# A transformer block on one core: the row of token scales sent to all partitions through HBM instead of by diagonals and matmuls

## The chip, the cores and the metric

The kernel runs on one core of a Trainium2 chip. The metric is the device time of one execution in microseconds (us). Five engines work side by side, each through its own list of instructions in order: TensorE (PE in the profile, with PEld for its weight loads), VectorE (DVE), ScalarE (ACT), GpSimd (POOL) and SyncE (SP), which here only issues DMAs. An engine waits for another by semaphores. GpSimd can issue DMAs too, on a queue of its own.

## The reference

A block with 256 tokens of 2048 features (all float32):

```python
h = rmsnorm(x, norm1_g)                        # per token: x * rsqrt(mean(x*x) + eps) * g
q, k, v, u = split(h @ w_in)                   # 12 query heads, 4 key/value heads, Fourier width 512
a = rmsnorm(window_attention(q, k, v, sink), attn_out_g)
f = rmsnorm(fourier_mix(u, w_fourier), fourier_out_g)
x = x + concat([a, f]) @ w_out
h = rmsnorm(x, norm2_g)
gate, val = split(h @ w_up)                    # 5504 columns each
gate = conv3(gate, dw_w) + dw_b                # along the tokens, each feature by itself
x = x + (gelu(gate) * val) @ w_down
y = rmsnorm(x, normf_g)
```

Each rmsnorm has one scale per token, 1/sqrt(mean square). Such a scale commutes with the matmul behind it, so the kernel multiplies the unscaled rows by the weights and applies the scale to the result.

## The kernel before, in words

**Products.** Every float32 product is split into three in a faster format: a weight tile `raw` becomes `hi` (a rounded copy, made by ACT in line 168) and `lo` (the rest, made by DVE in line 169), the tokens likewise, and PE adds hi·hi, lo·hi and hi·lo in PSUM. `split(i)` does this for the weight tile `i`, a "unit" of 128x2048, and then issues the load of unit `i + 3` on SP's queue (line 152), since there are three `raw` buffers. `hi` and `lo` also have three buffers each.

**Order.** All instructions are written out by hand in the order in which they are issued on each engine; no scheduler moves them. In the first part (attention, Fourier, output projection) `unit(i, work)` issues what is listed in `before[i]`, the matmuls of unit `i`, what is listed in `beside[i]`, the split of unit `i + 2`, and what is listed in `behind[i]`. In the second part (up-projection, convolution, down-projection) `ff_step(n)` does the same around item `n`: `beside[n]`, the split of item `n + 2`, `behind[n]`. Items 0, 1, 2, ... are gate 0, value 0, gate 1, value 1, gate 2, value 2 and so on; each is 32 matmuls by `still_weights` (line 319), 16 that use `hi` and 16 that use `lo`, in turn.

**Two layouts of the scale.** `rstd_of` (line 261) leaves the scales of the 256 tokens as a tile of 128 partitions x 2: token b·128+p sits in partition p, column b. DVE makes `var` (line 264) and POOL raises it to the power -0.5 (line 267). Where the result of a product has tokens along the partitions, this form is used directly. Where the result has features along the partitions and the tokens along the free dimension (the keys, and gate and value), the scale is needed as a row of 256 numbers that is the same in all 128 partitions: `r1b` for the first rmsnorm, `r2b` for the second.

**How the row is made before.** `spread_diagonals` (line 276) has DVE multiply the identity `ident` by each of the two columns, which gives two 128x128 diagonal matrices in a buffer of the tag `junk`. `spread_sums` (line 283) has PE multiply a matrix of `ones` by each diagonal (line 286); every row of the result in PSUM is then the row of scales. Each of these two products of float32 shows as two matmuls in the trace, so four for a row. DVE copies the result to SBUF: `r1b` in line 569, `r2b` in line 293.

**Where that stands.** For `r1b` the three pieces are spread over the steps: diagonals behind unit 6, matmuls before unit 8, copy beside unit 8; the first reader is the first key's `qk_out` (line 604), beside unit 9. For `r2b` all stands in one place (line 1126): after the matmuls of items 0 and 1 have been issued, DVE reduces the sums of squares (line 1125), `rstd_of` follows, then the diagonals, the matmuls and the copy, and then `ff_step(1)`, which splits item 3. PE goes on with item 2.

**Readers of r2b.** `scaled_sum` (line 829) adds the two halves of a finished item out of PSUM (ACT copies one half, DVE adds the other, line 833, which frees the PSUM bank) and multiplies by `r2b` (line 834). `gate_conv` (line 837) then works on the result: ACT in line 841, DVE in lines 842 and 845. `up_posts` (line 984) places these: the sum of item n beside n + 1, the convolution beside n + 2.

**GpSimd's list.** Around the two places it has the powers of line 267, additions of squares (line 456) in the first part, and from item 13 on DMAs that add weights (lines 947, 949, 958).

Of the kernel before, what the change touches and what calls it, by code (L numbers as in the profile page):

```python
# [8 lines left out]
F32 = mybir.dt.float32  # L9
F32R = mybir.dt.float32r  # L10
AF = mybir.ActivationFunctionType
ALU = mybir.AluOpType

P = 128
D = 2048
S = 256
# [76 lines left out]
def block_kernel(  # L93
# [18 lines left out]
    nc = tc.nc  # L112
# [3 lines left out]
    wp = ctx.enter_context(tc.tile_pool(name="wp", bufs=1))  # L116
    mm = ctx.enter_context(tc.tile_pool(name="mm", bufs=4, space=bass.MemoryType.PSUM))
    dn = ctx.enter_context(tc.tile_pool(name="dn", bufs=4, space=bass.MemoryType.PSUM))
# [4 lines left out]
    def bank(pool, name):  # L123
        return pool.tile([P, 512], F32, tag=pool.name, name=name)
# [115 lines left out]
    ones = base.tile([P, P], F32, tag="ones", name="ones")  # L240
# [3 lines left out]
    ident = base.tile([P, P], F32, tag="ident", name="ident")  # L244
    make_identity(nc, ident)

    ps = bank(dn, "ps_warm")
# [25 lines left out]
            junk, t[:, b, :], AF.Square, accum_out=parts[:, b, c : c + 1]  # L273
        )

    def spread_diagonals(r, name):
        t = wp.tile([P, 512], F32, tag="junk", name=f"diag{name}")
        dgs = [t[:, b * P : (b + 1) * P] for b in range(2)]
        for b, dg in enumerate(dgs):
            nc.vector.tensor_scalar(dg, ident, r[:, b : b + 1], None, ALU.mult)  # L280
        return dgs

    def spread_sums(dgs, name):
        ps = bank(dn, "ps_spread" + name)
        for b in range(2):
            nc.tensor.matmul(
                ps[:, b * P : (b + 1) * P], ones, dgs[b], start=True, stop=True
            )
        return ps

    def spread(r, dst, name):

        nc.vector.tensor_copy(dst, spread_sums(spread_diagonals(r, name), name)[:, :S])


    def moving_weights(hi, lo, n, kk, act, b, ps, first, last, q0=0):
# [45 lines left out]
    before, beside, behind = {}, {}, {}  # L342

    def at(when, i, f, *a):
        when.setdefault(i, []).append((f, a))
# [13 lines left out]
    for c in range(4):  # L359
        t = base.tile([P, 4, 512], F32R, tag=f"hT{c}", name=f"hT{c}")  # L360
        hT.append(t)
    ps_u = [bank(mm, f"ps_u{b}") for b in range(2)]
    for k in range(NK):
# [3 lines left out]
        n = 1 if c < 2 else 2  # L367
# [8 lines left out]
        if k < 4:  # L376

            for p, w in enumerate([hi, hi, lo]):
                for b in range(2):
# [3 lines left out]
                        start=k == 0 and p == 0, stop=False,  # L383
# [15 lines left out]
    r1 = base.tile([P, 2], F32, tag="rstd1", name="rstd1")  # L399
# [19 lines left out]
    def rows_out(hi, lo, ps):  # L419

        for b in range(2):
            r = r1[:, b : b + 1]
            nc.scalar.activation(hi[:, b, :], ps[b], AF.Copy, scale=r)
            nc.vector.scalar_tensor_tensor(
                lo[:, b, :], ps[b], r, f32(hi[:, b, :]), ALU.mult, ALU.subtract
            )
# [9 lines left out]
    r1b = ph.tile([P, S], F32, tag="r1b", name="r1b")  # L436
# [120 lines left out]
            nc.vector.tensor_scalar(rel[:, s], rel[:, s], rq_inv[:, b : b + 1], None, ALU.mult)  # L557
        nc.vector.tensor_scalar(sink_neg, vcol(V_SINK, NH), -1.0, None, ALU.mult)

    spread1 = {}  # L560
    at(beside, 5, fourier_positions)
    at(before, 6, fourier_weights)
    at(beside, 6, fourier_weights_out)
    at(behind, 6, lambda: spread1.update(d=spread_diagonals(r1, "1")))
    at(before, 7, fourier_rows)
    at(beside, 7, fourier_rows_out)
    at(before, 8, lambda: spread1.update(ps=spread_sums(spread1["d"], "1")))
    at(beside, 8, lambda: rows_out(v_hi, v_lo, ps_v))
    at(beside, 8, lambda: nc.vector.tensor_copy(r1b, spread1["ps"][:, :S]))
    at(behind, 8, distances)  # L570

    def fourier_channels_steps():
# [216 lines left out]
    for n, (c, kq) in enumerate(OUT_ORDER):  # L789
# [15 lines left out]
        if kq >= 2:  # L805
            part = "a" if kq == 2 else "f"
            ps = ps_a[c] if kq < 3 else ps_a[c, "f"]
# [18 lines left out]
    parts = {}  # L826
    gate_out, sums_of, act = {}, {}, {}

    def scaled_sum(ps, name):
        tmp = fp.tile([P, S], F32, tag="ftmp", name=f"ft_{name}")  # L830
        nc.scalar.activation(tmp, ps[:, S : 2 * S], AF.Copy)  # L831
        add = fp.tile([P, S], F32, tag="fadd", name=f"fa_{name}", bufs=3)
        nc.vector.tensor_tensor(add, ps[:, 0:S], tmp, ALU.add)  # L833
        nc.vector.tensor_tensor(add, add, r2b, ALU.mult)
        sums_of[name] = add

    def gate_conv(j):
        ga = sums_of.pop(f"g{j}")
# [144 lines left out]

    def up_posts(n, kind, j, ps):
        if kind == "gate":
            at(beside, n + 1, scaled_sum, ps, f"g{j}")
            at(beside, n + 2, gate_conv, j)
            at(behind, n + 2, gate_gelu, j)
        else:
            at(beside, n + 1, scaled_sum, ps, f"v{j}")  # L990
            at(beside, n + 2, val_mult, j)
            if j % 8 == 7 and j < 8 * N_GROUPS:
                g = j // 8
                at(behind, n + 1, operand, g, "P1")
                at(behind, n + 2, operand, g, "N4")
                at(behind, n + 3, operand_sums, g, 0)
                at(behind, n + 4, operand, g, "P7")
                at(behind, n + 4, operand, g, "P2")
                at(behind, n + 5, operand_sums, g, 1)
                at(behind, n + 5, operand, g, "N5")  # L1000
                at(behind, n + 6, operand, g, "N3")
                at(behind, n + 7, operand, g, "P6")
            if j >= 8 * N_GROUPS:
                at(behind, n + 2, act_parts, j)
# [108 lines left out]
    for q in range(2):  # L1113
        kind, j = items[q]
        ps = bank(mm, f"ps_{kind}{j}")
# [8 lines left out]
    tot2 = base.tile([P, 2], F32, tag="tot2", name="tot2")  # L1124
    nc.vector.tensor_reduce(tot2, ssq2, mybir.AxisListType.X, ALU.add)
    spread(rstd_of(tot2, D, "2"), r2b, "2")
    ff_step(1)
    up_posts(1, *items[0], pair[0][0])
    up_posts(2, *items[1], pair[1][0])

    for n, it in enumerate(items):
# [8 lines left out]
        if it[0] in ("gate", "val"):  # L1140
            kind, j = it
            ps = bank(mm, f"ps_{kind}{j}")
            still_weights(*halves.pop(up_index[n]), ps, range(NK))
            ff_step(n)
            up_posts(n, kind, j, ps)
            continue
        if it[0] == "product":
            kind, g, c, p = it
# [3 lines left out]
            else:  # L1152
                ps = bank(mm, f"ps_{p}{g}{c}")
# [5 lines left out]
        else:  # L1159
            kind, g, c = it  # L1160
            hi, lo = halves.pop(up_index[n])
            ps = [bank(mm, f"ps_l{g}{c}{b}") for b in range(2)]
# [160 lines left out]
```

## Time and profile before

| | |
|---|---|
| time, median of 3 runs | 948.39 us (948.16 to 949.04) |
| the profiled execution's own time | 948.77 us |
| its span, first to last instruction | 947.0 us |
| TensorE (PE) | 937.1 us busy, 5085 matmuls |
| VectorE (DVE) | 750.0 us busy |
| ScalarE (ACT) | 534.2 us busy |
| GpSimd (POOL) | 43.3 us busy, 58 instructions |
| moved by DMA | 211.58 MB, mean 223 GB/s |

The page gives for each engine the time in which it was busy, and then the chain that ended last: the work followed back from the last instruction, each time to what released it. A timeline gives one line per instruction: start, duration, engine, line of the kernel, operation, result <- operands, and in brackets the idle time ahead of it and what ended it. PE's matmuls are pipelined: the next starts before the last one's duration is over, so the difference of two starts, and not a duration, says what a matmul takes of PE's time.

### The profile page before, as it was taken

How to read it: one execution, taken by the hardware profiler on the slowest of the kernel's cores; microseconds unless marked ns; L12 is line 12 of the kernel's file. 1: busy time of each engine (PE TensorE's matmuls, PEld its weight loads, DVE VectorE, ACT ScalarE, POOL GpSimd, SP SyncE). 2: the span in 40 equal slices, each digit the busy share in tenths (PEclk: the TensorE clock that was granted, in tenths of full speed). 3: DMA queues.
4: the chain of work that ended last, by engine and by line, in shares of the span. 5: the costliest groups of instructions: out<-in, count | busy, mean ns of one | idle time of the engine just before them, and what ended most of it. 6: DMA issues, size and time to landing. Idle time of an engine off the chain costs nothing.

```text
span 947.0 us, 12779 instructions
## 1 busy us (share of the span) xinstructions
PE 937.1 (99%) x5085; PEld 813.0 (86%) x5085; DVE 750.0 (79%) x935; ACT 534.2 (56%) x646; POOL 43.3 (5%) x58
## 2 busy tenths in 40 slices
PE   9999999999999999999999999999999999999996
PEld 7889998888888888888888888888888888888885
DVE  7758877666676689887898877988879979888775
ACT  7756766454454546556565555665556755553442
POOL 0000000000000000000000000000000000000003
PEclk9999999999999999999999999999999999999998
DMA  9844444446446675987778797877987787776542
GB/s 366 337 181 141 174 139 172 139 173 219 181 178 226 248 237 185 282 250 263 229 257 246 237 304 235 267 231 227 296 256 245 207 301 219 224 242 220 179 133 89
DMA packets 32108, 211.58 MB, mean 223 GB/s; under 512 B 3504, under 2 KB 4016, under 8 KB 7984
## 3 DMA queue, kind: packets, MB, share of 16 engines
q1 hardware_dynamic: 28448, 184.55, 52.4%
q0 software_dynamic: 3600, 26.22, 14.7%
q8 instruction: 40, 0.66, 0.3%
q14 instruction: 20, 0.16, 0.0%
HBM read 208.65 MB, written 2.10 MB: 223 GB/s over the span
## 4 chain that ended last, share of the span: by engine, by line
PE 98%; DVE 1%; DMA 0%; issue 0%; ACT 0%; POOL 0%; POOLq 0%; DVEq 0%; ACTq 0%
PE ps_gate L319 25%; PE ps_val L319 25%; PE ps_q L319 7%; PE ps_P L1051 3%; PE ps_P L1053 3%; PE ps_P L1052 3%; PE ps_a L304 2%; PE ps_k L319 2%; PE ps_a L302 2%; PE ps_a L303 2%; PE ps_N L1051 2%; PE ps_N L1053 2%; PE ps_N L1052 2%; PE ps_l L303 2%; PE ps_l L302 2%; PE ps_l L304 2%
## 5 line engine op out<-in xcount | busy, mean ns | idle before, releaser
L169 DVE TENSOR_TENSOR lo<-raw,hi 128x2048 fp32r<-128x2048 f32 (+1 forms) x133 | 302.7, 2276 | 54.0 <-ACT hi L168 54.0
L168 ACT ACTIVATE hi<-raw 128x2048 fp32r<-128x2048 f32 (+1 forms) x133 | 253.1, 1903 | 59.2 <-PE ps_l L303 24.9
L319 PE MATMUL ps_gate<-hU,hi 128*128 128x512 f32 x688 | 236.2, 389 | 0.0
L319 PE MATMUL ps_val<-hU,hi 128*128 128x512 f32 x688 | 236.2, 389 | 0.0
L319 PE MATMUL ps_gate<-hU,lo 128*128 128x256 f32 x688 | 189.9, 276 | 0.0
L319 PE MATMUL ps_val<-hU,lo 128*128 128x256 f32 x688 | 189.9, 276 | 0.0
L319 PEld LDWEIGHTS ps_gate<-hU,hi 128*128 128x128 f32 x688 | 129.2, 188 | 26.8
L319 PEld LDWEIGHTS ps_val<-hU,hi 128*128 128x128 f32 x688 | 129.1, 188 | 26.8
L319 PEld LDWEIGHTS ps_gate<-hU,lo 128*128 128x128 f32 x688 | 129.1, 188 | 1.1
L319 PEld LDWEIGHTS ps_val<-hU,lo 128*128 128x128 f32 x688 | 129.2, 188 | 1.1
L831 ACT ACTIVATE ft_g<-ps_gate 128x256 f32<-128x256 f32 x43 | 16.5, 384 | 120.0 <-PE ps_gate L319 119.8
L319 PE MATMUL ps_q<-hT,hi 128*128 128x512 f32 x192 | 66.2, 392 | 0.0
L831 ACT ACTIVATE ft_v<-ps_val 128x256 f32<-128x256 f32 x43 | 16.5, 384 | 88.0 <-PE ps_val L319 88.0
L319 PE MATMUL ps_q<-hT,lo 128*128 128x256 f32 x192 | 52.5, 277 | 0.0
L1051 PE MATMUL ps_P<-hi_P,op_P 128*128 128x512 f32 x128 | 49.8, 389 | 0.0
L1052 PE MATMUL ps_P<-hi_P,op_P 128*128 128x512 f32 x128 | 49.8, 389 | 0.0
L1053 PE MATMUL ps_P<-lo_P,op_P 128*128 128x512 f32 x128 | 49.8, 389 | 0.0
L943 DVE TENSOR_TENSOR lo_N<-sumw,hi_N 128x2048 fp32r<-128x2048 f32 x16 | 36.6, 2290 | 10.2 <-ACT hi_N L942 10.2
L319 PEld LDWEIGHTS ps_q<-hT,hi 128*128 128x128 f32 x192 | 35.8, 188 | 7.0
L302 PE MATMUL ps_a<-hi,cat 128*128 128x512 f32 x96 | 37.9, 395 | 0.0
L304 PE MATMUL ps_a<-lo,cat 128*128 128x512 f32 x96 | 37.5, 391 | 0.0
L833 DVE TENSOR_TENSOR fa_g<-ps_gate,ft_g 128x256 f32<-128x256 f32 x43 | 18.2, 422 | 24.3 <-ACT ft_g L831 24.3
(332 smaller groups left out, 1606.0 us busy)
## 6 DMA issues: line engine op xcount, KB each, us to landing
raw<-in_w_up SPq DMA_DIRECT2D x86, 1024.0 KB, 5.2
raw<-in_w_in SPq DMA_DIRECT2D x20, 1024.0 KB, 4.8
raw<-in_w_out SPq DMA_DIRECT2D x16, 1024.0 KB, 4.8
sumw<-in_w_down POOLq DMA_DIRECT2D x16, 1024.0 KB, 8.7
raw<-in_w_down_late SPq DMA_DIRECT2D x8, 1024.0 KB, 4.8
raw<-in_w_down_last SPq DMA_DIRECT2D x4, 768.0 KB, 4.2
ux<-in_w_u_x SPq DMA_DIRECT2D x3, 768.0 KB, 9.3
xs<-in_x SPq DMA_DIRECT2D x4, 512.0 KB, 16.1
```

Of the source, the lines that this page charges most:

```text
L168: nc.scalar.activation(hi[:, 0:n], raw[:, 0:n], AF.Copy)
L169: nc.vector.tensor_tensor(lo[:, 0:n], raw[:, 0:n], f32(hi[:, 0:n]), ALU.subtract)
L302: nc.tensor.matmul(ps, ah, wh, start=first and q == q0, stop=False)
L303: nc.tensor.matmul(ps, al, wh, start=False, stop=False)
L304: nc.tensor.matmul(ps, ah, wl, start=False, stop=last and q == q0 + len(kk) - 1)
L319: nc.tensor.matmul(ps[:, x], (hi, lo)[i][:, k * P : (k + 1) * P], hk(k)[:, x], start=n == 0 and k == 0, stop=n == len(order) - 1 and k == ...
L831: nc.scalar.activation(tmp, ps[:, S : 2 * S], AF.Copy)
L833: nc.vector.tensor_tensor(add, ps[:, 0:S], tmp, ALU.add)
L943: nc.vector.tensor_tensor(lo, src, f32(hi), ALU.subtract)
L1051: nc.tensor.matmul(ps, o[:, 0, p, :], hi[:, s], start=first and p == 0, stop=False)
L1052: nc.tensor.matmul(ps, o[:, 1, p, :], hi[:, s], start=False, stop=False)
L1053: nc.tensor.matmul(ps, o[:, 0, p, :], lo[:, s], start=False, stop=last and p == 3)
```

## The change

The row of scales goes by way of HBM. POOL issues two DMAs: the first writes the 128x2 tile to a tile `row` of 2x128 numbers in HBM, element by element in the order of the tokens; the second, which waits for the first, reads these 256 numbers into each of the 128 partitions. The diagonals, the matmuls and the copies are gone, for `r1b` and for `r2b`. For `r1b` both DMAs stand behind unit 6. For `r2b` they stand where `spread` stood; besides, the first reader is moved: `scaled_sum` of gate 0 leaves out the multiplication by `r2b`, which is done in `row_scale` beside item 3, after the split of item 4, ahead of gate 0's convolution. All other readers stay as they are.

```diff
-    def spread_diagonals(r, name):
-        t = wp.tile([P, 512], F32, tag="junk", name=f"diag{name}")
-        dgs = [t[:, b * P : (b + 1) * P] for b in range(2)]
-        for b, dg in enumerate(dgs):
-            nc.vector.tensor_scalar(dg, ident, r[:, b : b + 1], None, ALU.mult)
-        return dgs
-
-    def spread_sums(dgs, name):
-        ps = bank(dn, "ps_spread" + name)
-        for b in range(2):
-            nc.tensor.matmul(
-                ps[:, b * P : (b + 1) * P], ones, dgs[b], start=True, stop=True
-            )
-        return ps
+    rows = ctx.enter_context(tc.tile_pool(name="rows", bufs=1, space=bass.MemoryType.DRAM))
 
     def spread(r, dst, name):
 
-        nc.vector.tensor_copy(dst, spread_sums(spread_diagonals(r, name), name)[:, :S])
+        row = rows.tile([2, P], F32, tag="row" + name, name="row" + name)
+        nc.gpsimd.dma_start(row.rearrange("b p -> p b"), r)
+        nc.gpsimd.dma_start(dst, row.rearrange("b p -> (b p)").partition_broadcast(P))
...
-    spread1 = {}
     at(beside, 5, fourier_positions)
     at(before, 6, fourier_weights)
     at(beside, 6, fourier_weights_out)
-    at(behind, 6, lambda: spread1.update(d=spread_diagonals(r1, "1")))
+    at(behind, 6, spread, r1, r1b, "1")
     at(before, 7, fourier_rows)
     at(beside, 7, fourier_rows_out)
-    at(before, 8, lambda: spread1.update(ps=spread_sums(spread1["d"], "1")))
     at(beside, 8, lambda: rows_out(v_hi, v_lo, ps_v))
-    at(beside, 8, lambda: nc.vector.tensor_copy(r1b, spread1["ps"][:, :S]))
     at(behind, 8, distances)
...
-    def scaled_sum(ps, name):
+    def scaled_sum(ps, name, late=False):
         tmp = fp.tile([P, S], F32, tag="ftmp", name=f"ft_{name}")
         nc.scalar.activation(tmp, ps[:, S : 2 * S], AF.Copy)
         add = fp.tile([P, S], F32, tag="fadd", name=f"fa_{name}", bufs=3)
         nc.vector.tensor_tensor(add, ps[:, 0:S], tmp, ALU.add)
+        sums_of[name] = add
+        if not late:
+            row_scale(name)
+
+    def row_scale(name):
+        add = sums_of[name]
         nc.vector.tensor_tensor(add, add, r2b, ALU.mult)
-        sums_of[name] = add
...
         if kind == "gate":
-            at(beside, n + 1, scaled_sum, ps, f"g{j}")
+            at(beside, n + 1, scaled_sum, ps, f"g{j}", j == 0)
+            if j == 0:
+                at(beside, n + 2, row_scale, "g0")
             at(beside, n + 2, gate_conv, j)
             at(behind, n + 2, gate_gelu, j)
```

## The prediction

> **What bounds the kernel now.** I read the busy times first, then the chain that ended last, then PE's list of waits.
>
> ```profile
> span 947.0 us, 12779 instructions
> PE 937.1 (99%) x5085; PEld 813.0 (86%) x5085; DVE 750.0 (79%) x935; ACT 534.2 (56%) x646; POOL 43.3 (5%) x58
> ...
> PE 98%; DVE 1%; DMA 0%; issue 0%; ACT 0%; POOL 0%; POOLq 0%; DVEq 0%; ACTq 0%
> ```
>
> ```profile
> PE ps_warm L249 <- POOL ones L241: 1.0, 1, 1.0
> PE ps_u L381 <- ACT hT L256: 0.4, 1, 0.4
> ```
>
> PE is 98% of the chain, and its whole list of waits is the second fence: two, 1.4 us together, both at the very start. So from then on to its last matmul PE runs without a pause, and the end moves with PE's own work: a matmul taken out moves it by that matmul's share, and work of DVE, ACT, POOL or the DMAs counts only where it becomes late enough to stop PE.
>
> **What the change takes from PE.** Four matmuls for each row. Their price is read from the starts of the neighbours in PE's timeline (start, duration, instruction), first for r1b, then for r2b:
>
> ```profile
> 53.26 0.39 PE L303 MATMUL ps_v<-hi,hT 128*128 128x512 f32 x1
> 53.49 0.40 PE L304 MATMUL ps_v<-lo,hT 128*128 128x512 f32 x1
> 53.72 0.61 PE L286 MATMUL ps_spread<-diag,ones 128*128 128x128 f32 x4
> 54.17 0.61 PE L531 MATMUL ps_y<-uf,G 128*128 128x129 f32 x4
> ```
>
> ```profile
> 268.24 0.39 PE L319 MATMUL ps_val<-hU,hi 128*128 128x512 f32 x1
> 268.47 0.28 PE L319 MATMUL ps_val<-hU,lo 128*128 128x256 f32 x1
> 268.59 0.61 PE L286 MATMUL ps_spread<-diag,ones 128*128 128x128 f32 x4
> 268.95 0.48 PE L319 MATMUL ps_gate<-hU,hi 128*128 128x512 f32 x1
> 269.26 0.28 PE L319 MATMUL ps_gate<-hU,lo 128*128 128x256 f32 x1
> ```
>
> At r1b the spread holds PE from 53.72 to 54.17: 0.45 us; without it ps_y starts at 53.72, one pitch of L304 (0.23, as from 53.26 to 53.49) after it. At r2b the undisturbed pair has 0.23 us from a hi matmul to its lo matmul (268.24 to 268.47) and 0.12 from there to the next hi. So without the spread the gate's hi would start at 268.59 and its lo at 268.82; it starts at 269.26, which is 0.44 late. The two together: **0.9 us**, on the path.
>
> **What it takes from DVE** is off the path: the diagonals, the copies and one wait.
>
> ```profile
> 46.23 0.48 DVE L280 TENSOR_SCALAR diag<-ident,rstd 128x128 f32<-128x128 f32 x2
> ...
> 55.31 0.41 DVE L569 COPY r1b<-ps_spread 128x256 f32<-128x256 f32 x1
> ```
>
> ```profile
> 266.03 0.48 DVE L280 TENSOR_SCALAR diag<-ident,rstd 128x128 f32<-128x128 f32 x2 [0.80 <-POOL rstd L267]
> 269.23 0.42 DVE L293 COPY r2b<-ps_spread 128x256 f32<-128x256 f32 x1 [2.72 <-PE ps_spread L286]
> 269.57 2.28 DVE L169 TENSOR_TENSOR lo<-raw,hi 128x2048 fp32r<-128x2048 f32 x1
> 271.77 0.42 DVE L833 TENSOR_TENSOR fa_g<-ps_gate,ft_g 128x256 f32<-128x256 f32 x1
> 272.23 0.42 DVE L834 TENSOR_TENSOR fa_g<-fa_g,r2b 128x256 f32<-128x256 f32 x1
> 272.57 2.29 DVE L169 TENSOR_TENSOR lo<-raw,hi 128x2048 fp32r<-128x2048 f32 x1
> 274.77 0.48 DVE L842 SCALAR_TENSOR_TENSOR cv<-fa_g,vec,cv 128x255 f32<-128x255 f32 x1
> ...
> 277.27 2.29 DVE L169 TENSOR_TENSOR lo<-raw,hi 128x2048 fp32r<-128x2048 f32 x1
> ```
>
> That is 1.8 us of work and 2.72 us in which DVE sat waiting for PE's spread. No wait of PE names DVE, so I count them at nothing. The cover is PE's own distance to the next tile that it needs, worked out below.
>
> **What it adds: two DMAs in a row on POOL, and a wait of DVE.** POOL computes the scales and then issues both; the second waits for the first. What starts, and what stands behind in POOL's list:
>
> ```profile
> 35.95 0.71 POOL L267 TENSOR_TENSOR rstd<-var,half_pow 128x2 f32<-128x2 f32 x1 [34.47 <-DVE var L264]
> 69.20 0.75 POOL L456 TENSOR_TENSOR sq_f<-sq_f,sq 128x256 f32<-128x256 f32 x1 [32.55 <-ACT sq L455]
> ...
> 265.31 0.69 POOL L267 TENSOR_TENSOR rstd<-var,half_pow 128x2 f32<-128x2 f32 x1 [64.73 <-DVE var L264]
> ```
>
> ```profile
> 336.51 1.05 POOL L958 DMA_DIRECT2D rawd00b<-in_w_down  x1 [70.52 <-DVE cv L842]
> ```
>
> POOL's next work is 32 us behind the first pair and 70 us behind the second, so POOL's own waiting holds up nobody. SP's queue is not passed by anything: its loads follow DVE's splits as before.
>
> What one such DMA takes, from issue to landing, the trace doesn't show: nothing in it writes single 4-byte elements to HBM, and nothing this small is issued by POOL. The nearest rows (tile, queue, KB, us to landing; then a POOL issue's own time in ns):
>
> ```profile
> gfb<-in_normf_g POOLq DMA_DIRECT2D x1, 1024.0 KB, 4.8
> ...
> out_y<-xs SPq DMA_DIRECT2D x2, 128.0 KB, 1.9
> ```
>
> ```profile
> rawd10b<-in_w_down POOLq DMA_DIRECT2D x1, 1024.0 KB, 10.1
> ```
>
> ```profile
> L1168 POOL DMA_DIRECT2D gfb<-in_normf_g x1: 568/568/568, 839.8 to 839.8; - x1
> ```
>
> The low end is 1.9 us each (SP, 128 KB, the size of the second DMA), the high end 10.1 us each (POOL's slowest, which adds 1 MB in place). I take 4.8 us each, gfb's: it is the one plain DMA from POOL, and like the second one it repeats an HBM row to all partitions, though eight times as many bytes. Its issue took POOL 0.57 us, which lies within. The pair is then 9.6 us, with ends at 3.8 and 20.2.
>
> The Trainium skill's page "DMA: Bandwidth & Descriptors", section "Anatomy of one DMA — SWDGE (gpsimd) path", gives about 2.0 us plus the bytes at 436 GB/s per DMA; by it the pair would take an estimated 4.3 us, near the low end, and the sum would be the same. The gfb row, 4.8 us for 1 MB, agrees with its 4.4.
>
> **r1b.** The scales are ready at 35.95 + 0.71 = 36.7; r1b lands at 46.3, or at 56.9 by the high end. Its first reader:
>
> ```profile
> 61.18 0.42 DVE L604 TENSOR_TENSOR add_k<-add_k,r1b 128x256 f32<-128x256 f32 x1
> ```
>
> That is 60.7 once PE is 0.45 us earlier. It is in time by either end: no cost.
>
> **r2b** is the one to watch. All of the following is the time of before less 0.45. The scales are ready at 265.31 + 0.69 - 0.45 = 265.55. DVE now does: the split of item 3 as soon as ACT's half is there, the sum of gate 0 (which frees the PSUM bank and doesn't need r2b), the split of item 4, then the late multiplication. ACT's and PE's rows for it:
>
> ```profile
> 267.31 1.91 ACT L168 ACTIVATE hi<-raw 128x2048 fp32r<-128x2048 f32 x1 [2.87 <-PE ps_gate L319]
> ...
> 272.68 0.60 ACT L841 ACTIVATE cv<-fa_g,vec 128x256 f32<-128x256 f32 x1 [1.38 <-DVE fa_g L834]
> ```
>
> ```profile
> 285.36 0.39 PE L319 MATMUL ps_val<-hU,hi 128*128 128x512 f32 x1
> 285.59 0.28 PE L319 MATMUL ps_val<-hU,lo 128*128 128x256 f32 x1
> ```
>
> Item 3's split starts at 267.31 + 1.91 - 0.45 = 268.8; with DVE's pitches above (2.20 for a split, 0.46 for the sum, 2.20 for the next split) it reaches the multiplication at **273.7**. r2b lands at 265.55 + 9.6 = 275.2 (ends 269.4 and 285.8). So DVE probably waits some 1.5 us here, in place of the 2.72 that it waited before.
>
> Behind that multiplication on DVE stand gate 0's convolution, the sums of value 0 and gate 1, and the split of item 5, value 2. If the multiplication starts at T, ACT's convolution part begins 0.45 later and takes 0.60, DVE goes on about 0.05 behind that, and from there it is 277.27 - 274.77 = 2.50 to the split and 2.29 through it: item 5 is ready at T + 5.9. PE needs its lo at 285.59 - 0.9 = 284.7. So PE stops only if r2b lands after **278.8**, 13.2 us behind the scales. With 9.6 there are 3.6 us to spare. The cost is nothing; by the high end it would be 285.8 - 278.8 = 7.0 us.
>
> **The sum.** Against the profiled execution, 947.0 of span and 1.8 around it, 948.8 in all: minus 0.9. It stands 0.4 above the median of the runs (948.39); the same difference there gives **947.5 us**, 0.1% less. A measurement of this kernel can tell about 0.2% (1.9 us) from no change, so this counts as no change.
>
> **The rivals.**
>
> *The second row is late (slower).* The place is DVE's late multiplication, with item 5's split behind it; it decides from 13.2 us for the pair on. At 10.1 us each PE stops for 7.0 us: 948.39 - 0.9 + 7.0 = 954.5. For it: 256 elements of 4 bytes are a kind of write of which the trace has no row, and two landings stand one behind the other. Against: POOL's 10.1 is for 1 MB that is added in place, and DMAs have room there, as the row below shows (columns: stretch and length, then busy time and count of PE, PEld, DVE, ACT, POOL, then granted clock, DMA share, GB/s).
>
> ```profile
> 268.00:274.00 6.00, 6.00 (x38) 5.37 (x37) 4.73 (x5) 4.17 (x5) 0.00 (x0) 1.00 0.19 41
> ```
>
> A variant is that descriptors of POOL's DMAs wait for DVE's splits: one split of 2.29 us ahead of each DMA adds 4.6, so r2b lands at 279.8 and PE stops for 1.0, which gives 948.5, still within 0.2%. The Trainium skill, page "SBUF — State Buffer", section "Who interferes with whom", has DVE shut GpSimd out for a whole instruction, but only copies, casts and tensor_scalar in their two-port modes, and it notes that tensor_tensor did not stall DMAs. By that the variant falls; no row of before can show it.
>
> *Nothing is gained: 948.4.* PE's 0.9 us comes back as a wait, if the stream of split weights and not PE sets the pace, or if ps_y and the gate start no earlier. For it: PE would be 0.9 us closer to every load and split. Against: PE's list has no wait for DVE, ACT or a DMA after the start, and the item at 285.36 had its split done at 279.6.
>
> *More is gained.* If DVE's time did set the pace somewhere, its 2.72 of idle time goes too: 948.39 - 0.9 - 2.72 = 944.8. The same list speaks against it.
>
> **How the numbers follow.** The forecast has 0.79; nothing gained 0.08; late row 0.09; more gained 0.04. The forecast and the second give "within 0.2%", 0.87; late row is slower, 0.09; more gained is faster, 0.04. The range runs from 946.8 (the forecast less 0.45, an error of half the PE term, and less the 0.2 by which the fastest run lies below the median) to 949.1 (nothing gained, plus the 0.65 by which the slowest run of before lies above its median); it takes in the short stop of 1.0 us, and leaves out the full late row and the larger gain.
>
> **What will show it.** In the profile after: PE's busy time about 1 us less, its waits still two, ps_y 0.23 us behind the last L304, and the gate 0.12 behind the last value matmul. r2b's multiplication for gate 0 starts between 273.7 and 276, with an idle time of 0 to 3 us ahead of it that ends on the DMA. What would prove me wrong: an idle time of over 5 us there and a PE wait for a hi or lo of line 168 or 169 at about 284.5; or a PE wait anywhere else.

## The result, and the profile after

The changed kernel takes **954.42 us** (median of 6 runs, 953.17 to 956.27), against 948.41 for the kernel before on the same days (6 runs): ratio **1.0064, 95% interval 1.0054 to 1.0074**. It is 6.0 us slower, where 0.9 us faster was forecast. Some executions of e4_act_queue, e5_early and e7_filler were about 15 us longer than the others of the same kernel, with matmuls a little slower for hundreds of us; the medians below leave them out, and of the profiles of e5 and e7, which fell into such executions, only the stretch up to 292 us is read. Lines of `kernel.py` have moved: the weights' matmuls of line 319 now stand in line 308, the multiplication by r2b in 826.

The busy times and PE's list of waits of the changed kernel; the profiled execution took 956.27 us:

```profile
span 954.5 us, 12766 instructions
PE 940.5 (99%) x5077; PEld 815.3 (85%) x5077; DVE 748.0 (78%) x929; ACT 534.1 (56%) x646; POOL 45.7 (5%) x62
```

```profile
PE ps_val L308 <- DVE lo L169: 2.0, 1, 2.0
PE ps_val L308 <- ACT hi L168: 1.9, 1, 1.9
PE ps_warm L249 <- POOL ones L241: 1.0, 1, 1.0
PE ps_u L370 <- ACT hT L256: 0.7, 1, 0.7
```

Two waits are new, both at one item, value 2. PE has 8 matmuls fewer and is nevertheless busy for 3.4 us longer. The reason for the waits is read on POOL and on DVE:

```profile
266.12 0.69 POOL L267 TENSOR_TENSOR rstd<-var,half_pow 128x2 f32<-128x2 f32 x1 [64.73 <-DVE var L264]
267.11 0.76 POOL L281 DMA_DIRECT2D row<-rstd  x1 [0.29 <-POOL rstd L267]
277.08 0.57 POOL L282 DMA_DIRECT2D r2b<-row  x1 [9.22 <-DMA row<-rstd]
```

```profile
270.07 2.29 DVE L169 TENSOR_TENSOR lo<-raw,hi 128x2048 fp32r<-128x2048 f32 x1 [4.03 <-ACT hi L168]
...
272.61 2.28 DVE L169 TENSOR_TENSOR lo<-raw,hi 128x2048 fp32r<-128x2048 f32 x1
284.30 0.43 DVE L826 TENSOR_TENSOR fa_g<-fa_g,r2b 128x256 f32<-128x256 f32 x1 [9.41 <-DMA r2b<-row]
...
287.91 2.28 DVE L169 TENSOR_TENSOR lo<-raw,hi 128x2048 fp32r<-128x2048 f32 x1
```

The scales are ready at 266.81 and r2b is used at 284.30, **17.5 us** later. DVE sits for 9.41 us ahead of that multiplication, and item 5's split, behind it, ends only at 290.2. ACT's half of that split comes late too, since it stands behind gate 0's convolution in ACT's list: that is PE's first wait, of 1.9 us; the wait for DVE's half ends last. The DMAs of that stretch (last column: us from issue to landing):

```profile
raw<-in_w_up SPq DMA_DIRECT2D x3, 1024.0 KB, 9.4
r2b<-row POOLq DMA_DIRECT2D x1, 128.0 KB, 7.1
row<-rstd POOLq DMA_DIRECT2D x1, 1.0 KB, 9.3
```

One KB takes 9.3 us to land and the 128 KB behind it 7.1. Of the three weight loads the first was issued ahead of the row and took 4.9 us; the two issued at 272.39 and 274.92, while the row was on its way, took 9.4 and 11.1, and the same two took 5.6 and 5.0 before. What the DMA engines did in the meantime (columns: stretch and length, busy time and count of PE, granted clock, DMA share, GB/s):

```profile
268.00:269.00 1.00, 1.00 (x8) 1.00 0.05 1
269.00:270.00 1.00, 1.00 (x8) 1.00 0.00 0
273.00:274.00 1.00, 1.00 (x7) 1.00 4.24 131
```

This view counts a packet wholly in the stretch in which it starts. The row's 16 packets of 64 bytes, and 16 more of 4 bytes, all run between 268.47 and 268.67 (the DMA packets of the trace); the row lands at 276.4. So the sending is short, and the time passes between it and the landing. No other packet starts until 273.37, when the load of 272.39 begins; its first 16 packets take 3.0 to 5.7 us each, where one of this size takes 0.31 in quiet stretches. They are held, and not slowed by other traffic: none is under way. What holds them is left to the experiments.

The granted clock (columns as in the prediction's row of 268 to 274):

```profile
286.00:292.00 6.00, 2.26 (x7) 1.75 (x8) 5.86 (x11) 5.97 (x7) 0.00 (x0) 0.78 0.13 26
292.00:298.00 6.00, 6.00 (x26) 5.13 (x26) 5.97 (x7) 2.97 (x4) 0.00 (x0) 0.66 0.76 287
```

In these two stretches, which hold PE's waits and the 6 us behind them, the granted clock is 0.78 and 0.66. PE's own rows around it:

```profile
285.60 0.28 PE L308 MATMUL ps_gate<-hU,lo 128*128 128x256 f32 x1
287.76 0.50 PE L308 MATMUL ps_val<-hU,hi 128*128 128x512 f32 x1 [1.88 <-ACT hi L168]
290.24 0.58 PE L308 MATMUL ps_val<-hU,lo 128*128 128x256 f32 x1 [1.98 <-DVE lo L169]
290.62 0.63 PE L308 MATMUL ps_val<-hU,hi 128*128 128x512 f32 x1
...
298.33 0.39 PE L308 MATMUL ps_gate<-hU,hi 128*128 128x512 f32 x1
```

The account of this execution, by starts against before: value 2 begins 2.04 us late (287.76 for 285.72), its first lo another 2.25 late (290.24 for 287.99), and from there to the next item PE takes 8.09 us for what takes 5.21 at full clock, 2.88 more. That is 7.2 us. The two spreads give 0.9 back, and PE's beginning was 1.3 us later in this execution (line 302's first matmul, now line 291, starts at 12.63 for 11.34): PE waited 0.3 longer for its first `hT`, and the first matmuls kept a pitch of some 0.46 us, in place of 0.23, for longer, which makes 1.0. Together +7.6; the spans differ by 7.5. Without that beginning it is +6.3, and the medians differ by 6.0. The matmuls behind the two former spreads start as the prediction said: ps_y 0.23 us behind the last matmul ahead of it (55.01 for 54.78), the gate 0.11 behind the value (269.39 for 269.28).

### The profile page after: what moved, and what is told of

It is laid out like the page before. It is cut to its first block, busy times and chain, and to the rows that moved or that the text cites. A ratio compares the mean times of both kernels' runs of the same rounds, so it can differ in the third digit from the quotient of the medians.

```text
span 954.5 us, 12766 instructions
## 1 busy us (share of the span) xinstructions
PE 940.5 (99%) x5077; PEld 815.3 (85%) x5077; DVE 748.0 (78%) x929; ACT 534.1 (56%) x646; POOL 45.7 (5%) x62
## 4 chain that ended last, share of the span: by engine, by line
PE 95%; DMA 2%; DVE 1%; ACT 0%; issue 0%; POOL 0%; POOLq 0%; DVEq 0%; ACTq 0%
PE ps_val L308 24%; PE ps_gate L308 23%; PE ps_q L308 7%; PE ps_P L1045 3%; PE ps_P L1044 3%; PE ps_P L1046 3%; PE ps_a L293 2%; PE ps_a L291 2%; PE ps_k L308 2%; PE ps_a L292 2%; PE ps_N L1045 2%; PE ps_N L1046 2%; PE ps_N L1044 2%; PE ps_l L293 2%; PE ps_l L292 2%; PE ps_l L291 2%
## 5 line engine op out<-in xcount | busy, mean ns | idle before, releaser
L308 PE MATMUL ps_val<-hU,hi 128*128 128x512 f32 x688 | 238.9, 392 | 1.9 <-ACT hi L168 1.9
L934 DVE TENSOR_TENSOR lo_N<-sumw,hi_N 128x2048 fp32r<-128x2048 f32 x16 | 36.6, 2290 | 10.2 <-ACT hi_N L933 10.2
L291 PE MATMUL ps_a<-hi,cat 128*128 128x512 f32 x96 | 37.9, 395 | 0.0
L292 PE MATMUL ps_a<-hi,cat 128*128 128x512 f32 x96 | 37.3, 389 | 0.0
```

Of the source, the lines that this page charges most:

```text
L291: nc.tensor.matmul(ps, ah, wh, start=first and q == q0, stop=False)
L292: nc.tensor.matmul(ps, al, wh, start=False, stop=False)
L308: nc.tensor.matmul(ps[:, x], (hi, lo)[i][:, k * P : (k + 1) * P], hk(k)[:, x], start=n == 0 and k == 0, stop=n == len(order) - 1 and k == ...
L934: nc.vector.tensor_tensor(lo, src, f32(hi), ALU.subtract)
```

## The experiments

The theory after the result, **element writes**: writing 256 elements of 4 bytes side by side into HBM is slow by itself and holds up the DMA engines for others; so r2b is late. "Side by side" means that the elements follow one another in HBM without a gap. Rivals: **GpSimd's queue** (each of its DMAs costs 7 to 9 us), **traffic** (weight loads beside it), and descriptors (the entries that tell the DMA engines what to move) that wait for DVE. Two of these the changed kernel's own trace speaks against, as far as the row is concerned: when the row was issued at 267.11 no load was under way (the last had landed at 266.7, the next was issued at 272.39), and DVE sat idle for 4.03 us up to 270.07, while all packets of the row had run by 268.67. Times are medians, with the ratio to the kernel before measured beside it; most of these kernels differ from the changed kernel (C) by the edit shown; e2 and e3 leave out the second rmsnorm's scale. Differences below 0.2% between the faster versions are not told apart here.

| run | us | ratio, 95% interval |
|---|---|---|
| changed kernel | 954.42 | 1.0064 (1.0054 to 1.0074) |
| e1_pairs | 947.35 | 0.9990 (0.9981 to 0.9999) |
| e2_row512 | 947.63 | 0.9993 (0.9984 to 1.0002) |
| e3_no_row | 947.52 | 0.9992 (0.9982 to 1.0001) |
| e4_act_queue | 954.72 | 1.0065 (1.0048 to 1.0081) |
| e5_early | 948.24 | 1.0003 (0.9994 to 1.0012) |
| e6_only_r1 | 947.89 | 0.9995 (0.9987 to 1.0004) |
| e7_filler | 951.93 | 1.0038 (1.0024 to 1.0052) |
| e8_no_late | 955.93 | 1.0079 (1.0066 to 1.0092) |
| e10_best | 947.51 | 0.9991 (0.9982 to 1.0000) |

### e1_pairs: 8 bytes from each partition

```diff
-    spread(rstd_of(tot2, D, "2"), r2b, "2")
+    r2 = rstd_of(tot2, D, "2")
+    row2 = rows.tile([P, 2], F32, tag="row2", name="row2")
+    nc.gpsimd.dma_start(row2, r2)
+    nc.gpsimd.dma_start(r2b, row2.rearrange("p b -> (p b)").partition_broadcast(P))
...
-        nc.vector.tensor_tensor(add, add, r2b, ALU.mult)
+        by_b = add.rearrange("p (b t) -> p b t", b=2)
+        nc.vector.tensor_tensor(by_b, by_b, r2b.rearrange("p (t b) -> p b t", b=2), ALU.mult)
```

> The second row is written to HBM as it lies in SBUF, 8 bytes from each partition (128 pieces in place of 256 of 4 bytes), and DVE reads r2b with a stride of two to put the tokens in order. Theory, element writes: the changed kernel's row takes 9.3 us because each 4-byte element is a write of its own, some 0.03 us each one behind the other; with half as many the row lands in about 5.3 us, r2b behind it in 4 to 6, the pair in about 11 us in place of 17.5; that is inside the 13.2 us that PE allows, so no wait of PE for item 5 and 947.5 us. Rival, GpSimd's queue: a DMA issued by POOL costs 7 to 9 us whatever it holds; pair 17.5 us, 954.4. Rival, traffic: both are held up by the weight loads beside them; also unchanged, 954.4.

```profile
r2b<-row POOLq DMA_DIRECT2D x1, 128.0 KB, 3.7
row<-rstd POOLq DMA_DIRECT2D x1, 1.0 KB, 3.2
```

The same KB lands in 3.2 us for 9.3, less than the 5.3 that half the number of writes would give, and r2b in 3.7 for 7.1. PE has no wait behind its start and the time is 947.35. "Every DMA from POOL is slow" falls, and so does traffic as the cause of the row's 9.3: the same weight loads are issued at the same places. DVE reads with a stride of two at the old price (0.42 us).

### e2_row512 and e3_no_row: two pieces of 512 bytes, or no write

```diff
+        nc.gpsimd.dma_start(row2, ones[0:2, :])
...
+    nc.gpsimd.dma_start(r2b, normf_g[0:S].partition_broadcast(P))
```

The first line is e2's, in place of the scales; the second is e3's only DMA for this row.

> The second row's first DMA writes two contiguous pieces of 512 bytes, taken from the matrix of ones: the second rmsnorm's token scale is left out (it is 1). Same place in POOL's list, same second DMA. Theory, element writes: row lands in 2 to 3 us, r2b in 3 to 5, 947.5 us. Rivals, GpSimd's queue and traffic: row still about 9 us and r2b 7, 954.4.

> The second row's first DMA is left out: r2b is read from 256 numbers of an input that have been in HBM from the start (the second token scale is left out and replaced by these). Theory, element writes: without them nothing blocks the DMA engines, r2b lands 3 to 5 us behind its issue in place of 7.1, and the weight load issued at about 272.4 takes about 5 us in place of over 9; 947.5 us. Rival, GpSimd's queue: r2b still takes about 7 us, the weight load beside it 5; 947.5 us as well, so it is told apart by the durations. Rival, traffic: r2b falls to about 3 us because no load is in flight at 267, and the load at 272.4 takes 5 us.

e2, then e3:

```profile
r2b<-row POOLq DMA_DIRECT2D x1, 128.0 KB, 3.2
row<-ones POOLq DMA_DIRECT2D x1, 1.0 KB, 1.6
```

```profile
raw<-in_w_up SPq DMA_DIRECT2D x7, 1024.0 KB, 4.8
r2b<-in_normf_g POOLq DMA_DIRECT2D x1, 128.0 KB, 3.4
```

With two long pieces the row lands in 1.6 us, and the pair takes 4.8; without the write r2b takes 3.4 and the weight loads 4.8. So the loads' 9.4 and 11.1 in the changed kernel come from the row write. r2b's 7.1 follows from it at least in part by way of the loads: r2b is issued only at 277.08, behind the two held loads, and its packets start at 281.6, whereas e3's r2b is issued with no load under way. How much of the 7.1 is common queueing isn't separated; in e10, where the first row is written in pairs, r1b took 6.1 us with a load issued 1.5 us ahead of it.

### e4_act_queue: the same elements from ACT's queue

```diff
-    spread(rstd_of(tot2, D, "2"), r2b, "2")
+    r2 = rstd_of(tot2, D, "2")
+    row2 = rows.tile([2, P], F32, tag="row2", name="row2")
+    nc.scalar.dma_start(row2.rearrange("b p -> p b"), r2)
+    nc.gpsimd.dma_start(r2b, row2.rearrange("b p -> (b p)").partition_broadcast(P))
```

> The same 256 elements of 4 bytes as the second row, but issued by ACT on its own hardware queue instead of by POOL; the second DMA stays on POOL. Theory, element writes: the row still lands about 8 to 9 us behind its issue, r2b in about 7, 954 us. Rival, GpSimd's queue: row falls to 2 to 3 us, the pair to about 10, 947.5 us. Rival, traffic: as in the changed kernel, 954.

```profile
r2b<-row POOLq DMA_DIRECT2D x1, 128.0 KB, 7.0
row<-rstd ACTq DMA_DIRECT2D x1, 1.0 KB, 9.4
```

Nothing changes: 9.4 and 7.0, 954.72 us. It is not GpSimd's queue; and descriptors of POOL that wait for DVE are not needed for it either, since a write that POOL doesn't issue is as slow.

### e5_early: the same two DMAs, begun earlier

```diff
             ff_step(0)
+            tot2 = base.tile([P, 2], F32, tag="tot2", name="tot2")
+            nc.vector.tensor_reduce(tot2, ssq2, mybir.AxisListType.X, ALU.add)
+            spread(rstd_of(tot2, D, "2"), r2b, "2")
             turn_x(3)
...
-    tot2 = base.tile([P, 2], F32, tag="tot2", name="tot2")
-    nc.vector.tensor_reduce(tot2, ssq2, mybir.AxisListType.X, ALU.add)
-    spread(rstd_of(tot2, D, "2"), r2b, "2")
```

> The changed kernel with one move: the sum of squares, the power and both DMAs of the second row stand ahead of the transposition of the last quarter of the tokens on DVE and POOL, where the squares are just done; the two DMAs are the same 4-byte elements as in the changed kernel. Theory, r2b is late: the scales are ready at about 260.9 in place of 265.5, the pair takes the same 16 to 17.5 us, r2b lands at 277 to 278.4, which is inside the 278.8 that PE allows; 947.5 us, up to 948.5 if it lands a little behind. Rival, the blocked DMA engines stop PE by themselves, through the weight loads that they hold up: nothing is gained by the move, about 954 us, with PE waiting for a split whose load landed late.

```profile
260.55 0.69 POOL L267 TENSOR_TENSOR rstd<-var,half_pow 128x2 f32<-128x2 f32 x1 [60.76 <-DVE var L264]
261.54 0.76 POOL L281 DMA_DIRECT2D row<-rstd  x1 [0.29 <-POOL rstd L267]
271.68 0.56 POOL L282 DMA_DIRECT2D r2b<-row  x1 [9.39 <-DMA row<-rstd]
```

```profile
PE ps_val L308 <- DVE lo L169: 1.2, 1, 1.2
```

The row is as slow as before, but starts 5.6 us earlier. r2b is used at 279.79, 1.0 behind the 278.8 of the prediction, and PE waits for 1.2 us at the predicted place (its beginning was 0.3 us earlier in this execution than in the trace of before). The time is 948.24 (11 executions, 946.97 to 950.86), within what was expected: the cost is r2b's lateness, and not what the held engines do to the weight loads.

### e6_only_r1: the first row alone

C's `spread` for r1b, the diagonals and matmuls of before for r2b.

> Only the first row goes by way of HBM; the second is made by diagonals and matmuls as before, with its first reader where it was. Theory: r1b lands at about 54, 7 us ahead of its reader, so only PE's 0.45 us is gained: 947.95 us. The element writes hold up weight loads here as well, which may take 0.3 to 0.6 us of that back through a late split: up to 948.5. Rival, the blocked loads cost PE: over 950.

```profile
raw<-in_w_in SPq DMA_DIRECT2D x6, 1024.0 KB, 9.7
r1b<-row POOLq DMA_DIRECT2D x1, 128.0 KB, 7.2
row<-rstd POOLq DMA_DIRECT2D x1, 1.0 KB, 8.8
```

947.89 us, 0.40 less than before beside it, near the 0.45 of one spread. The interval takes in no change, so the size agrees with the expectation and isn't shown by the time alone. The loads here are held up as well (9.7 us is the median of six; the three issued while the row was on its way or just behind it took 10.9 to 11.0), and PE has no wait for them.

### e7_filler: PE kept busy

```diff
             still_weights(*halves.pop(up_index[n]), ps, range(NK))
+            if n == 4:
+                for _ in range(20):
+                    nc.tensor.matmul(
+                        held[0, "P1"][:, 0:P], ones, ones, start=True, stop=True
+                    )
```

> The changed kernel with 20 matmuls of ones added behind item 4 on PE, into a PSUM bank that is begun afresh later (extra work whose result isn't used), some 4.5 us at 0.22 each, as long as PE waits for item 5. Theory, PE's idle time makes the granted clock fall (0.66 to 0.78 in the 12 us behind the wait, some 2.9 us lost): with PE kept busy the clock stays at 1.0 and the time falls to about 951.6 us. Rival, the clock falls for another reason (the weight loads, DVE and ACT at work together): the clock falls all the same, 954.4 us or a little more.

```profile
286.00:292.00 6.00, 5.60 (x40) 4.99 (x40) 5.90 (x10) 5.97 (x9) 0.00 (x0) 1.00 0.29 87
```

r2b is as late as in the changed kernel, PE does 4.6 us of useless work, and the kernel is 2.5 us faster than the changed one (951.93). The granted clock is 1.00 where it was 0.78 (the row's columns: PE, PEld, DVE, ACT, POOL, then clock), and over the whole of the three undisturbed executions it is 0.997, for 0.993 to 0.996 in the changed kernel. So some 2.5 to 2.9 of the 6.9 us that the changed kernel lost against the forecast were no waiting, but slow matmuls that the waiting brought about. The Trainium skill, page "TensorE: Matmul & The Clock Gate", section "Part 1: The HAM clock gate", says that the array's clock halves after an idle window of about 3.4 us and recovers after as much busy time. The fall agrees, the recovery takes longer here. In the changed kernel PE's last matmul at full speed ends at 285.9; read in stretches of 1 us, the clock is 1.00 up to 289 and 0.50 from 290 to 296. It falls some 3.4 us into the two pauses, although a matmul stands between them and neither pause alone is longer than 2.25 us. Matmuls run again from 290.24, at pitches of 0.43 and 0.21 us in place of 0.23 and 0.12, and the full clock is back only 5.9 us later.

### e8_no_late: the first reader where it was

```diff
-            at(beside, n + 1, scaled_sum, ps, f"g{j}", j == 0)
-            if j == 0:
-                at(beside, n + 2, row_scale, "g0")
+            at(beside, n + 1, scaled_sum, ps, f"g{j}")
```

> The changed kernel without the move of the first reader: gate 0 is multiplied by r2b ahead of the split of item 4, as before. Theory, r2b is late: DVE now waits ahead of item 4's split, so PE stops one item earlier and longer, for about 6.5 us in place of 4.3, plus the same 2.9 us of slow clock: about 957 us. If the late reader were what made the changed kernel slow, this would be faster than 954.4.

```profile
PE ps_gate L308 <- DVE lo L169: 5.8, 1, 5.8
```

955.93 us: PE now waits at item 4, for 5.8 us in one piece. The clock falls 3.3 us after PE has stopped and is full again 4.3 us after it goes on; by starts PE loses 6.0 us by the pause and 2.2 by slow matmuls, a little less than the 6.5 and 2.9 expected. The move of the reader is worth about 1.5 us here; it hides a part of the lateness, and isn't the cause of it.

### e9_forms, e11_idle and e12_owner: what makes such a write slow

> The best version below with six extra writes to HBM from GpSimd's queue, one by one behind units 15 to 26, whose results aren't used: dense (the changed kernel's 256 elements of 4 bytes, in the order of the tokens), half (128 such elements, one column), pair (128 pieces of 8 bytes), apart (256 elements of 4 bytes, but the two of a partition side by side, as in pair), pitch64 and pitch512 (256 elements of 4 bytes, 64 and 512 bytes from one to the next). Only their issue and landing are read, not the time of the kernel. If what costs is the number of small writes: dense, apart, pitch64 and pitch512 take 8 to 10 us each, half about 5, pair 3 to 5. If what costs is that neighbours within some tens of bytes are written by different DMA engines and wait for each other: dense 8 to 10, half 5 or more, apart, pitch64 and pitch512 only 2 to 4, like pair at 3.2.

In e9 the landings were 9.4 us for dense, 8.5 for half, 9.8 for pair, 8.2 for apart, 6.9 and 2.3 for the two pitches. This fits neither expectation: half is too slow for the first, apart for the second. Besides, pair and pitch64 stood behind a weight load for some 5 us before their first packet; counted from that packet on (the DMA packets of the trace), dense, half and apart took 7.4, 7.4 and 6.9 us, pair 4.1, the pitches 1.6 and 1.0. So the same was measured without loads:

```diff
+            probe("pitch64", ssq3[:, 0, 0:4:3], 16)    # 256 elements, 64 bytes apart
+            probe("pitch32", r1, 8)
+            probe("pitch16", r1, 4)
+            probe("pitch8", r1, 2)
+            probe("dense", r1)                         # the changed kernel's row
+            probe("half", r1[:, 0:1], 1, 1)            # 128 elements
```

> The best version with nine extra writes of 4-byte elements to HBM from GpSimd's queue near the end, when no load is under way, each waiting for the one before; their results aren't used, and the outputs come some 40 us later for them, so only their durations are read. In order: 256 elements 64, 32, 16 and 8 bytes apart, 256 side by side (the changed kernel's row), 128 side by side, 128 pieces of 8 bytes, 256 elements of 4 bytes with the two of a partition side by side, and 256 elements 64 bytes apart once more. If writes that share a block of 64 bytes go one behind the other, at about 0.46 us each (7.36 us for 16 in the run before), they land about 1.4 + 0.46 x (writes in one block) us behind their issue, no less than 2.3: 2.3, 2.3, 3.2, 5.1, 8.8, 8.8, 5.1, 8.8, 2.3. If the number of writes counts: 9 for all with 256, 5 for the 128. If it was the loads beside them: 2 to 3 for all.

Each waits for the one before, so the distance of two issues is the time of one, with 0.3 us on top:

```profile
926.12 0.77 POOL L1200 DMA_DIRECT2D scratch<-ssq  x1
928.41 0.75 POOL L1200 DMA_DIRECT2D scratch<-rstd  x1 [1.53 <-DMA scratch<-ssq]
930.70 0.72 POOL L1200 DMA_DIRECT2D scratch<-rstd  x1 [1.54 <-DMA scratch<-rstd]
932.95 0.72 POOL L1200 DMA_DIRECT2D scratch<-rstd  x1 [1.53 <-DMA scratch<-rstd]
937.02 0.72 POOL L1200 DMA_DIRECT2D scratch<-rstd  x1 [3.35 <-DMA scratch<-rstd]
946.20 0.57 POOL L1200 DMA_DIRECT2D scratch<-rstd  x1 [8.46 <-DMA scratch<-rstd]
955.67 0.55 POOL L1211 DMA_DIRECT2D scratch<-rstd  x1 [8.90 <-DMA scratch<-rstd]
959.77 0.67 POOL L1212 DMA_DIRECT2D scratch<-ssq  x1 [3.56 <-DMA scratch<-rstd]
967.41 0.72 POOL L1200 DMA_DIRECT2D scratch<-rstd  x1 [6.96 <-DMA scratch<-ssq]
```

256 elements that lie 64, 32 or 16 bytes apart take 2.3 us; 8 bytes apart 4.1; side by side **9.2**. 128 side by side take no less, 9.5. 128 pieces of 8 bytes take 4.1; 256 elements of which the two of a partition are neighbours, 7.6; the ninth, 64 bytes apart once more, landed in 2.0 like the first. Neither the number of writes nor the loads decide, then, but how densely they lie: 8 pieces in 64 bytes take 4.1 us whether a piece is 4 or 8 bytes long. My rule of 0.46 us for each write in a block of 64 bytes has the right order, but the steps are not even (four in a block cost nothing).

> As the run before, with five extra writes of 256 elements of 4 bytes, in order: 64 bytes apart; 16 elements of each of 16 partitions side by side, a block of 64 bytes for each partition; the same elements the other way round, so that each block of 64 bytes holds one element of each of the 16 partitions; the changed kernel's row; and the second once more. Only durations are read. If what costs is that different DMA engines write into one block: 2.0 us, about 2, 9 or more, 8.9, about 2. If what costs is the number of writes into one block, whoever makes them: 2.0, about 9, about 9, 8.9, about 9.

```profile
926.50 0.77 POOL L1201 DMA_DIRECT2D scratch<-ssq  x1
928.80 0.60 POOL L1205 DMA_DIRECT2D scratch<-ones  x1 [1.53 <-DMA scratch<-ssq]
937.64 0.59 POOL L1206 DMA_DIRECT2D scratch<-ones  x1 [8.25 <-DMA scratch<-ones]
945.96 0.74 POOL L1207 DMA_DIRECT2D scratch<-rstd  x1 [7.73 <-DMA scratch<-ones]
954.66 0.59 POOL L1208 DMA_DIRECT2D scratch<-ones  x1 [7.96 <-DMA scratch<-rstd]
```

With each block written from one partition 8.8 us, with each block written from all 16 partitions 8.3, the changed kernel's row 8.7; the second once more landed in 9.1 (8.6 the first time). From how many partitions a block is filled makes no difference that counts; how many writes fall into one small stretch of HBM does. Which DMA engine serves which partition no view shows. How wide that stretch is, and what happens in it, these runs don't settle.

### e10_best: dense pieces avoided, and begun early

Both rows as in e1, and e5's move.

> Both rows written as 8 bytes from each partition and read by DVE with a stride of two, and the second row's scales, with both DMAs, ahead of the last transposition on DVE and POOL. Theory: no DMA is blocked, r2b lands about 8 us before it is needed, PE keeps the 0.9 us: 947.4 us, as e1_pairs or 0.1 less. If the stride costs DVE time that matters, it would be slower than e1_pairs.

947.51 us, ratio 0.9991: with e1 (0.9990) the best version, and not to be told from it. r2b lands at about 270.5, and PE's list holds only waits of its beginning. The forecast 0.9 us of the matmuls explains the gain; starting earlier as well gains nothing more, since e1 was already in time.

## Why the prediction was wrong

**PE's 0.9 us: right.** Where the row comes in time, the whole change gives 0.7 to 1.0 us (e1, e2, e3, e10), and the first row alone 0.40 (e6). These are differences of medians near the edge of their intervals; the starts of ps_y and of the gate, 0.23 and 0.11 us behind their neighbours, show it in the trace.

**r1b at no cost: right**, e6; even though its pair took 17 us and not the 9.6 assumed, and its row held up the loads.

**How PE comes to stop: right.** Place, order of DVE's work and limit were as worked out: 13.2 us behind the scales. What the prediction named as the sign of being wrong is what came: 9.41 us of idle time ahead of the multiplication, where it said over 5, and PE's waits for lines 168 and 169 from 285.9 on. With the measured 17.5 the formula gives 17.5 - 13.2 = 4.3 us; PE lost 2.04 + 2.25 = 4.29. In e5 the split was ready at 285.68, as T + 5.9 gives (279.79 + 5.9), and PE, which had begun 0.3 earlier, waited 1.2 where the formula has 1.0. Left out was that ACT's half of the split is late too; it ended first, so it changed nothing.

**Wrong: "I take 4.8 us each, gfb's".** The pair took 17.5 us, not 9.6, of which 9.3 and 7.1 were the landings. It lay inside my ends of 3.8 and 20.2, and the late row was a rival, but with a chance of 0.09. The error was to choose the nearest row by queue and form of the copy. What counted was the one thing that I had noted and given no price, that the trace has no write of single 4-byte elements. And the two DMAs were treated as if each stood alone: the second was issued behind two weight loads that the first had held up (3.4 with no load under way, e3). By the rule of the Trainium skill that the prediction weighed (page "DMA: Bandwidth & Descriptors", section "Anatomy of one DMA — SWDGE (gpsimd) path": 2.0 us and the bytes at 436 GB/s), the pair is an estimated 4.3 us. e2's landings, 1.6 + 3.2 = 4.8, bear that out for pieces of 512 bytes; the changed kernel's, 9.3 + 7.1 = 16.4, contradict it for dense elements.

**Left out: the slow clock.** The price of a late row was put at its wait alone. The wait brought 2.9 us of half-speed matmuls with it (e7), two fifths of the loss. With 17.5 us for the pair the sum would have been 948.4 - 0.9 + 4.3 + 2.9 = 954.7; measured 954.4. That the late-row rival's 954.5 lies so near is luck: it had a pair of 20.2 us, a stop of 7.0 and no slow clock.

**The range** had its upper end at 949.1, because the whole case of the late row was left outside. An unknown term whose upper end (20.2) lies beyond the limit that decides (13.2) deserved more than one chance in eleven.

## What to carry to other kernels

A tile that is moved by a small DMA should leave in pieces that are as long as the layout allows: permuting on the reading side (a stride on DVE) was free here, while single elements side by side cost 6 us more (9.3 for 3.2) and held up the weight loads issued beside them. When a step has an operation that the trace doesn't show, price it by what sets it apart, and ask whether its upper end crosses the point at which the busy engine stops. And a wait of the busy engine costs more than its length, if the engine's clock falls behind it, as it did after pauses of 4.3 us in all and not after one of 1.2 (e5).

## What the runs showed of the hardware

- 256 writes of 4 bytes into HBM take 2.3 us if they lie 16 bytes or more apart, 4.1 at 8 bytes, 9.2 side by side; 128 side by side take 9.5 (issue to next issue, no loads under way).
- While the dense ones are under way, other DMAs of the core are held: weight loads issued then landed in 9.4 and 11.1 us, for 5.6 and 5.0 of the same loads before; their first packets took 3.0 to 5.7 us, for 0.31. With the write issued by ACT they took 9.0 and 10.2.
- The packets of such a write are sent within 0.2 us; the landing comes 7.7 us behind the last of them (changed kernel, second row).
- After two pauses of PE, 4.3 us by starts with one matmul between them, and after one of 5.8 us (e8), the granted clock was 0.50 for some 6.8 us, from 3.4 and 3.3 us after PE stopped; after one of 1.2 us (e5), and with PE kept busy (e7), it stayed at 1.00.
